# A two-layer hybrid encoder in split fp32r products: one PSUM bank per turned memory column, later casts for the second memory layer, split scores for the memory heads

## The chip, the cores and the metric

The kernel runs on one core of one Trainium2 chip. The metric is the device time of one execution in microseconds (us), the median of the runs shown. The core has a matrix engine (TensorE, PE; its weight loads appear as PEld), a vector engine (VectorE, DVE), an engine for activations and scaled copies (ScalarE, ACT), a general engine (GpSimd, POOL) and a sync engine that issues transfers (SyncE, SP). Each engine works through its own instructions in a fixed order. Matrix products are summed in PSUM, whose banks of 128 x 512 fp32 are the accumulators. DMA transfers move data between the chip's large memory and SBUF.

## What is computed

The reference is a trunk of two layers (DEPTH 2) over a sequence of 256 tokens of width 2048, with 256 memory tokens of the same width. What matters here of one layer:

```
proj = rmsnorm(x, norm_g[l]) @ w_in[l]            # split into conv, diff-attention and memory parts
y_a  = short_gated_conv(a_x, a_b, a_c, ...) * silu(a_g)
y_d  = headRMS(softmax(Q1 K1 / 8 + alibi) V - lam * softmax(Q2 K2 / 8 + alibi) V) * silu(d_g)   # 6 heads

mkv  = rmsnorm(mem, mem_norm_g[l]) @ w_mem_kv[l]  # 256 x 1024: keys | values
mk   = rmsnorm(mkv[..., :512] by heads of 128, mem_k_norm_g[l])
mv   = mkv[..., 512:] by heads of 128
mq   = rmsnorm(m_q by heads of 128, mem_q_norm_g[l])
y_m  = softmax(mq mk^T / sqrt(128)) mv * silu(m_g)                                              # 4 heads

x = x + concat(y_a, y_d, y_m) @ w_out[l]
```

All is fp32. The memory tokens are the same in both layers, so the keys and values of both can be made first.

## The kernel before

**Split products.** A large fp32 product is made of three products in fp32r, a shorter fp32 format with the size of fp32. Each operand is split into `hi`, its fp32r rounding (a cast on ACT), and `lo`, the rest (a subtraction on DVE). `products` (L298 to 304) then issues hi x hi, hi x lo and lo x hi for a 128 x 512 accumulator, 128 rows of the inner dimension at a time; the matmuls stand in L302. With two row tiles of 128 tokens that is six matmuls for each 128 x 512 piece of weights.

**Weights.** They arrive in `raw` tiles of 128 x 1024 (four buffers), are cast to `hi` and `lo` (four buffers each), and are read by PE. A buffer of `hi` and `lo` is free again when PE has done its products, a buffer of `raw` when DVE has made `lo`.

**The memory phase** comes first (class `Memory`, and the loop behind it). Its step s is layer l = s // 16 and inner tile k = s % 16: 0 to 15 are layer 0, 16 to 31 layer 1. A step has one `raw` tile of w_mem_kv: half 0 for the keys, half 1 for the values. Both halves and both row tiles make four accumulators, and the pool of accumulators has four banks, so layer 1's four are the banks of layer 0's four. `load` issues a step's transfer, `make` casts it: `hi` in L773 with the norm's gain as the scale, `lo` in L774. `times` runs the products. The loop takes steps in ones, and in pairs at k = 14, 15 and k = 0, 1, and makes the casts of the next steps ahead of a step's products.

When layer 0 is through, `keep_keys` (L872) copies the two key accumulators to `kraw` on ACT (L875), and `keep_values` (L878) copies the two value accumulators to `mv`, with a scale, on ACT (L880). Layer 1's first product into a bank has to wait for that bank's copy. The keys are then normed by pieces that run beside the next steps (squares in L359, the rest on DVE), turned by way of memory outside the core in `keys` (L718) into `mkT`, and multiplied there by the gain of the key norm, 128 x 1024 on ACT (L731).

Memory tokens come in rows and have to be turned: `rows_T` (L613) lets PE transpose two columns of 128 into one PSUM tile `pt` (L619), a bank, from a pool of two banks; `split_T` casts each column into `memT`, hi on ACT (L258), lo on DVE (L259). The first layer's steps do this; the second finds `memT` complete.

**What sets the order.** The framework orders each engine's instructions by its own simulated timeline, except those under `pin` (tc.keep_in_program_order), which stay in the order of the code relative to one another. Pinned are, among others, the copies of keys and values and the casts of steps up to 17 (`if s < KT + 2`, KT = 16). The casts of later steps are put where the framework's timeline has them.

**The layers** follow: per layer 14 blocks of 512 columns of w_in, then w_out. Each block takes its weights 128 x 1024 at a time ("chunk", 12 matmuls, about 2.7 us on PE). The small work runs beside the blocks as generators; `yield n` lets n chunks pass. The memory heads' queries are normed and turned into `mqT`, after which `turn_mq` marks the layer in `queries`. `mem_scores` (L589) waits for that mark and issues two fp32 matmuls for each head, `s<-mkT,mqT`, 128x256 (L595; the profile has two records for each). Softmax, the product with the values (L442, `po`), and a turn of the output by way of memory follow; `split_T` casts the outputs into `yT`, the stationary operand of w_out. The first two blocks of w_out start with the ten inner tiles of the diff and memory heads and take those of the convolution later.

The tile with tag `bgT` holds the turned gates of the convolution later in the layer; the tag has one buffer, and earlier in the layer the diff heads' second keys `k2` lie in it.

Of the kernel before, what the change touches and what calls it, by code (L numbers as in the profile page):

```python
# [10 lines left out]
F32 = mybir.dt.float32  # L11
F32R = mybir.dt.float32r
I32 = mybir.dt.int32
AF = mybir.ActivationFunctionType
ALU = mybir.AluOpType
# [3 lines left out]
P = 128  # L19
D_MODEL = 2048  # L20
SEQ = 256
DEPTH = 2
NT = SEQ // P
KT = D_MODEL // P
# [4 lines left out]
DH = W_DIFF // P  # L29
# [18 lines left out]
def encoder(ctx: ExitStack, tc: tile.TileContext, x, mem, norm_g, w_in, conv_w, conv_b,  # L48
            dq_g, dk_g, lq1, lk1, lq2, lk2, head_g, mem_norm_g, w_mem_kv, mq_g, mk_g, w_out, out):
    nc = tc.nc  # L50
    x, mem, out = x[0], mem[0], out[0]

    def pool(name, bufs, space=None):
        kw = {"space": space} if space is not None else {}
        return ctx.enter_context(tc.tile_pool(name=name, bufs=bufs, **kw))
# [4 lines left out]
    keep = pool("keep", 1)  # L60
# [5 lines left out]
    ps_t = pool("ps_t", 2, PSUM)  # L66
# [3 lines left out]
    def nm(s):  # L70
        uid[0] += 1
        return f"{s}_{uid[0]}"


    ident = const.tile([P, P], F32, name="ident")
# [59 lines left out]
    def g_mnorm(l, k):  # L135
        return cva[:, l * KT + k:l * KT + k + 1]
# [4 lines left out]
    mgain = const.tile([P, DEPTH], F32, name="mgain")  # L141
# [138 lines left out]
    def parts_tiles():  # L280
        return [wp.tile([P, CK, NB], F32R, tag=tag, name=nm(tag), bufs=PARTS // CK) for tag in ("hi", "lo")]
# [134 lines left out]
    def carry(sheet, to):  # L416


        d = dram.tile([NA, B, NA, sheet.shape[-1]], F32, name=nm("d"))
        for a in range(NA):  # L420
            tc.keep_in_program_order(nc.sync.dma_start(d[:, :, a].rearrange("b c r -> c b r"), sheet[a * B:(a + 1) * B]))
        yield 2
        of = d.rearrange("b c a (n i) -> (b c) a n i", i=B)
        for a in range(NA):
            tc.keep_in_program_order(nc.sync.dma_start(to[:, :, a], of[:, a]))
# [71 lines left out]
    scored = set()  # L497
# [3 lines left out]
    def pair(heads, begin, end, v):  # L501

        es = []
        for h in heads:
            while held["e"] == 2:
                yield 1
            held["e"] += 1
            es.append((yield from begin(h)))
            yield 2
        yield 4  # L510
        while held["sh"] == 2:
            yield 1
        held["sh"] += 1
        sh = tmp.tile([P, NA, 2, NT * NT, B], F32, tag="sh", name=nm("sh"))
        for i, e in enumerate(es):
            tc.keep_in_program_order(nc.vector.transpose(
                sh[:, :, i], e[0].rearrange("p t (k b c) -> p b (t k) c", k=NT, b=NA)))
            held["e"] -= 1
            yield 1
        yield 4  # L520
        flat = sh.rearrange("p b h n c -> p (b h n c)")
        yield from carry(sh.rearrange("p b h n c -> p b (h n c)"), flat.rearrange("p (n a i) -> p n a i", a=NA, i=B))
        eT = flat.rearrange("p (h t k q) -> p h t k q", h=2, t=NT, k=NT)
        while held["yn"] == 2:
            yield 1
        held["yn"] += 1
        yn = tmp.tile([P, NA, 2, NT, B], F32, tag="yn", name=nm("yn"))
        for i, h in enumerate(heads):
            end[0](h, yn[:, :, i], weighted(eT, i, v, h), *es[i][1:])
            yield 2  # L530
        held["sh"] -= 1
        yield 5
        tc.keep_in_program_order(nc.vector.transpose(yn, yn))
        yield 5
        flat = yn.rearrange("p b h t c -> p (b h t c)")
        yield from carry(yn.rearrange("p b h t c -> p b (h t c)"), flat.rearrange("p (n a i) -> p n a i", a=NA, i=B))
        for i, h in enumerate(heads):
            end[1](h, flat[:, i * SEQ:(i + 1) * SEQ])
            yield 1
        held["yn"] -= 1  # L540
# [43 lines left out]
            nc.vector.scalar_tensor_tensor(yn[:, :, i], strips(po[:, i, :]), r[:, i:i + 1],  # L584
                                           strips(a[:, i, h * P:(h + 1) * P]), ALU.mult, ALU.mult)

    queries = set()

    def mem_scores(l, h, qT, kT, st):  # L589
        while l not in queries:  # L590
            yield 1
        sc = P ** -0.5
        s = ps_s.tile([P, NT, SEQ], F32, tag="s", name=nm("s"))
        for i in range(NT):
            nc.tensor.matmul(s[:, i, :], qT[:, h, i * P:(i + 1) * P], kT[:, h, :], start=True, stop=True)  # L595
        mx = small.tile([P, NT], F32, tag="mmx", name=nm("mmx"))
        nc.vector.tensor_reduce(mx, s, AX.X, ALU.max)
        nc.vector.tensor_scalar(mx, mx, -sc, None, ALU.mult)
        sm = small.tile([P, NT], F32, tag="msm", name=nm("msm"))
        e = tmp.tile([P, NT, SEQ], F32, tag="e", name=nm("me"))  # L600
        for i in range(NT):
            nc.scalar.activation(e[:, i], s[:, i], AF.Exp, bias=mx[:, i:i + 1], scale=sc, accum_out=sm[:, i:i + 1])
        r = small.tile([P, NT], F32, tag="mr", name=nm("mr"), bufs=6)
        nc.vector.reciprocal(r, sm)
        nc.vector.tensor_tensor(r, r, st[:, HR], ALU.mult)
        return e, r
# [5 lines left out]

    def rows_T(src, k, n):  # L613

        pt = ps_t.tile([P, 2, SEQ], F32, tag="t", name=nm("pt"))
        for j in range(n):
            for t in range(NT):
                tc.keep_in_program_order(
                    nc.tensor.transpose(pt[:, j, t * P:(t + 1) * P], src(k + j, t), ident))  # L619
        return [pt[:, j, :] for j in range(n)]  # L620

    def strips_of(src):

# [62 lines left out]
    pin = tc.keep_in_program_order  # L686
# [31 lines left out]
    def keys(l, nat):  # L718


        d = dram.tile([NA, B, NA, W_MEM // P * NT * B], F32, name=nm("kd"))
        flat = nat.rearrange("p b j t c -> p b (j t c)")
        for a in range(NA):
            tc.keep_in_program_order(nc.gpsimd.dma_start(d[:, :, a].rearrange("b c r -> c b r"), flat[a * B:(a + 1) * B]))
        tc.keep_in_program_order(nc.gpsimd.dma_start(flat, d.rearrange("b c a r -> (b c) a r")))
        yield 8
        tc.keep_in_program_order(nc.vector.transpose(
            mkT[l].rearrange("p j (t a i) -> p (j t) a i", t=NT, a=NA),
            nat.rearrange("p a j t c -> p (j t) a c")))
        yield  # L730
        tc.keep_in_program_order(nc.scalar.activation(mkT[l], mkT[l], AF.Copy, scale=mgain[:, l:l + 1]))  # L731

    def x_natural(q):
        pin(nc.sync.dma_start(xs[:, :, q * NB:(q + 1) * NB],
# [2 lines left out]
    class Memory:  # L737
# [20 lines left out]
        def make(self, s):  # L758
            if s in self.parts:
                return  # L760
            self.load(s)
            l, k = divmod(s, KT)
            raw, (hi, lo) = self.raw.pop(s), parts_tiles()
            self.parts[s] = hi, lo
            if l == DEPTH:
                both = (nc.scalar.copy(hi, raw), nc.vector.tensor_tensor(lo, raw, hi.bitcast(F32), ALU.subtract))
                if k < 2:
                    for i in both:
                        pin(i)
                return  # L770
            g = g_mnorm(l, k)
            for j in (range(2) if s < 2 else (slice(0, 2),)):
                both = (nc.scalar.activation(hi[:, j], raw[:, j], AF.Copy, scale=g),  # L773
                        nc.vector.scalar_tensor_tensor(lo[:, j], raw[:, j], g, hi[:, j].bitcast(F32),  # L774
                                                       ALU.mult, ALU.subtract))
                if s < KT + 2:
                    for i in both:
                        pin(i)

# [5 lines left out]
        def begin(self, half, part, w):  # L785

            if part == 0 and w == 0:
                self.acc[0, half] = accumulators()
            w_part = self.parts[0][w][:, half]
            for t in range(NT):  # L790
                pin(nc.tensor.matmul(self.acc[0, half][t], memT[:, part, 0, t * P:(t + 1) * P], w_part,  # L791
                                     start=part == 0 and w == 0, stop=False))
# [15 lines left out]
    mkT, mv, stm, away = [], [], [], []  # L808
# [80 lines left out]
    s = 1  # L889
    while s < DEPTH * KT:  # L890
        l, k = divmod(s, KT)
# [22 lines left out]
        s = group[-1] + 1  # L914

    for l in range(DEPTH):
        st = stats_of(ssx, "st")
# [11 lines left out]
        def begin_pair(n, p):  # L929
            tasks.append(later(p, max(1, start + PAIR_EVERY * n - chunk[0])))  # L930
# [4 lines left out]
        for b in order:  # L935
# [7 lines left out]
            if b == 4:  # L943
                start = chunk[0]
# [18 lines left out]
        mqT = keep.tile([P, MH, SEQ], F32, tag="mqT", name=nm("mqT"))  # L963
# [2 lines left out]

        def turn_mq(nat):
            yield from turn_sheet(nat, mqT)
            queries.add(l)

        tasks.append(later(turn_mq(normed(acc, P, st, sheets("bgx"))), 8))
        acc = x_block([(C_M + W_MEM, NB)])
# [4 lines left out]
            split_T(yT, CG + DH + h, y, None, pin=True)  # L977

        for n in range(MH // 2):
            begin_pair(DH // 2 + n, pair((2 * n, 2 * n + 1), lambda h: mem_scores(l, h, mqT, mkT[l], st),  # L980
                                         (lambda h, yn, po, r: mem_out(h, yn, po, r, mga), mem_done), mv[l]))


# [1 line left out]
        bgT = None  # L985
# [78 lines left out]
        for b in range(4):  # L1064
# [3 lines left out]
            for t in range(NT):  # L1068
                n = 256 if final else NB
# [41 lines left out]
```

## Time and profile before

| | us |
|---|---|
| runs: 928.17, 926.55, 927.01; median | 927.01 |
| the profiled execution | 929.68 |
| its span, first to last instruction | 927.9 |
| PE busy in it | 919.7 |
| DVE busy | 668.2 |
| ACT busy | 495.1 |
| matmuls on memory tokens, layer 1's first to the first on xT | 57.48 to 103.14 |

The profile is of one execution. A row of the timeline has the start and duration in us, the engine, the line of the kernel, the operation with output <- input by the program's names, the shape, a count, and in brackets the idle time of the engine before it with what ended that. Rows of the groups have a count, the busy time and the mean of one in ns. Matmuls overlap: the time between the starts of two is what counts, not the duration of one. "PEclk" is the clock that TensorE was granted, as a share of full speed. A table of waits has, for each pair of waiting line and releaser, the us in total, how often, and the longest.

### The profile page before, as it was taken

To read this page: it belongs to the slowest core of one execution; us is meant where nothing else is said; L and a number is where in the kernel's file an instruction comes from. 1 tells how busy PE (TensorE), PEld (TensorE's weight loads), DVE (VectorE), ACT (ScalarE), POOL (GpSimd) and SP (SyncE) were. 2 spreads that over 40 slices of the span, in tenths; PEclk is the share of its full clock that TensorE was granted. 3 is DMA by queue.
4 is the path that set the end of the run, shared out by engine and by line. 5 is a ranking of instruction groups with operands and counts; after the bars stand their busy time and mean duration, and the time that the engine had idled before them with its cause. 6 is when DMAs were issued, how large, how long until landed. Compare 5 with 4: busy or idle time off the path is not lost.

```text
span 927.9 us, 12263 instructions
## 1 busy us (share of the span) xinstructions
PE 919.7 (99%) x4168; PEld 763.6 (82%) x4168; DVE 668.2 (72%) x1176; ACT 495.1 (53%) x751; POOL 36.5 (4%) x66
## 2 busy tenths in 40 slices
PE   9989999999999999999999999999999999999998
PEld 6878888888888888888888888888888888888886
DVE  5569887857798786567666757878898777558652
ACT  5657645576454554445555544568554554446431
POOL 2335010000000000000000000000000000000000
PEclk9999999999999999999999999999999999999999
DMA  8888777875679998988587766886889879988662
GB/s 282 283 241 245 247 260 229 248 227 182 197 209 227 259 253 240 251 256 255 204 279 244 233 192 219 241 234 181 246 230 220 261 210 259 248 236 240 211 218 74
DMA packets 247023, 215.10 MB, mean 232 GB/s; under 512 B 132131, under 2 KB 172913, under 8 KB 246961
## 3 DMA queue, kind: packets, MB, share of 16 engines
q1 hardware_dynamic: 242080, 208.71, 76.2%
q0 software_dynamic: 3680, 4.56, 2.3%
q10 hardware_dynamic: 1200, 1.07, 0.4%
q8 instruction: 32, 0.52, 0.2%
q14 instruction: 31, 0.25, 0.1%
HBM read 193.26 MB, written 20.97 MB: 231 GB/s over the span
## 4 chain that ended last, share of the span: by engine, by line
PE 97%; DMA 2%; DVE 1%; ACT 1%; issue 0%; SPq 0%; DVEq 0%; ACTq 0%
PE acc L302 92%; PE po L442 2%; DMA raw<-in_w_mem_kv_dram 2%; PE s L595 1%; PE s L550 1%; PE s L549 1%; PE acc L791 1%; DVE lo L774 0%; ACT hi L773 0%; PE pt L619 0%; ACT msq L698 0%; ACT kraw L875 0%; DVE memT L259 0%; SPq L689 0%; DVE xs L1072 0%
## 5 line engine op out<-in xcount | busy, mean ns | idle before, releaser
L302 PE MATMUL acc<-hi,xT 128*128 128x512 f32 x1792 | 561.2, 391 | 0.0
L291 ACT CAST hi<-raw 128x1024 fp32r<-128x1024 f32 x280 | 294.4, 1052 | 342.8 <-PE acc L302 284.3
L292 DVE TENSOR_TENSOR lo<-raw,hi 128x1024 fp32r<-128x1024 f32 x280 | 341.9, 1222 | 182.2 <-ACT hi L291 177.0
L302 PEld LDWEIGHTS acc<-hi,xT 128*128 128x128 f32 x1792 | 336.7, 188 | 68.7
L302 PE MATMUL acc<-lo,xT 128*128 128x512 f32 x896 | 349.3, 390 | 0.0
L302 PEld LDWEIGHTS acc<-lo,xT 128*128 128x128 f32 x896 | 168.5, 188 | 33.9
L302 PE MATMUL acc<-hi,yT 128*128 128x512 f32 x512 | 158.0, 389 | 0.0
L302 PEld LDWEIGHTS acc<-hi,yT 128*128 128x128 f32 x512 | 96.2, 188 | 19.8
L302 PE MATMUL acc<-lo,yT 128*128 128x512 f32 x256 | 99.7, 389 | 0.0
L302 PE MATMUL acc<-hi,memT 128*128 128x512 f32 x248 | 78.4, 399 | 2.4 <-ACT kraw L875 2.4
L302 PEld LDWEIGHTS acc<-hi,memT 128*128 128x128 f32 x248 | 46.9, 191 | 12.4 <-ACT kraw L875 2.8
L302 PEld LDWEIGHTS acc<-lo,yT 128*128 128x128 f32 x256 | 48.1, 188 | 10.0
L774 DVE SCALAR_TENSOR_TENSOR lo<-raw,cva,hi 128x1024 fp32r<-128x1024 f32 (+1 forms) x34 | 40.9, 1219 | 15.9 <-ACT hi L773 15.5
L302 PE MATMUL acc<-lo,memT 128*128 128x512 f32 x124 | 46.9, 394 | 0.0
L773 ACT ACTIVATE hi<-raw,cva 128x1024 fp32r<-128x1024 f32 (+1 forms) x34 | 36.2, 1095 | 11.9 <-DMA raw<-in_w_mem_kv_dram 8.8
L302 PEld LDWEIGHTS acc<-lo,memT 128*128 128x128 f32 x124 | 23.7, 192 | 5.0
L560 ACT ACTIVATE e<-e,mx 128x256 f32<-128x256 f32 x48 | 23.8, 498 | 1.4 <-DVE mx L556 1.3
L636 POOL DMA_DIRECT2D xt<-in_x_dram x32 | 21.5, 678 | 20.1 <-DVE rsa L186 14.9
L404 DVE STREAM_TRANSPOSE sh<-sh 128x1024 f32<-128x1024 f32 (+2 forms) x14 | 17.3, 1238 | 0.0
L554 DVE SCALAR_TENSOR_TENSOR e<-dist,s 128x512 f32<-128x512 f32 x24 | 15.7, 679 | 2.2 <-PE s L550 1.7
L261 ACT ACTIVATE xT<-xf,gx 128x256 fp32r<-128x256 f32 x32 | 14.4, 502 | 4.1 <-DVE xf L642 3.5
L1072 DVE TENSOR_TENSOR xs<-acc,xs 128x256 f32<-128x256 f32 (+1 forms) x24 | 10.9, 504 | 7.8 <-PE acc L302 7.8
(161 smaller groups left out, 581.7 us busy)
## 6 DMA issues: line engine op xcount, KB each, us to landing
raw<-in_w_in_dram SPq DMA_DIRECT2D x192, 512.0 KB, 4.4
raw<-in_w_out_dram SPq DMA_DIRECT2D x64, 512.0 KB, 4.4
raw<-in_w_in_dram SPq DMA_DIRECT2D x64, 256.0 KB, 4.1
raw<-in_w_mem_kv_dram SPq DMA_DIRECT2D x30, 512.0 KB, 5.9
d<-sh SPq DMA_DIRECT2D x80, 128.0 KB, 3.8
sh<-d SPq DMA_DIRECT2D x64, 128.0 KB, 4.3
d<-yn SPq DMA_DIRECT2D x40, 64.0 KB, 3.8
yn<-d SPq DMA_DIRECT2D x40, 64.0 KB, 3.7
```

The source lines that it names most:

```text
L261: both = (nc.scalar.activation(hi, src, AF.Copy, scale=gain), nc.vector.scalar_tensor_tensor(lo, src, gain, hi.bitcast(F32), ALU.mult, ALU ...
L291: nc.scalar.copy(hi, raw)
L292: nc.vector.tensor_tensor(lo_, raw, hi.bitcast(F32), ALU.subtract)
L302: i = nc.tensor.matmul(acc, left, right, start=start, stop=stop)
L404: tc.keep_in_program_order(nc.vector.transpose(src, src))
L442: nc.tensor.matmul(po[:, t, :], eT[:, i, t, k, :], v[:, k, h * P:(h + 1) * P], start=k == 0, stop=k == NT - 1)
L554: nc.vector.scalar_tensor_tensor(e[:, c], dist, -slopes[h], s[c], ALU.mult, ALU.add)
L560: nc.scalar.activation(e[:, c, i], e[:, c, i], AF.Exp, bias=mx[:, c, i:i + 1], accum_out=sm[:, c, i:i + 1])
L636: tc.keep_in_program_order(nc.gpsimd.dma_start(st[:, n], src[n * B:(n + 1) * B].rearrange("p (b r) -> b p r", b=NA)))
L773: both = (nc.scalar.activation(hi[:, j], raw[:, j], AF.Copy, scale=g), nc.vector.scalar_tensor_tensor(lo[:, j], raw[:, j], g, hi[:, j].bit ...
L774: nc.vector.scalar_tensor_tensor(lo[:, j], raw[:, j], g, hi[:, j].bitcast(F32), ALU.mult, ALU.subtract))
L1072: nc.vector.tensor_tensor(xc, acc[t][:, lo:lo + n], xc, ALU.add)
```

## The change

It has three parts.

1. `rows_T` takes one PSUM tile, a bank, for each turned column, instead of one for two columns. The pool still has two banks.
2. The casts of steps 18 and 19 are pinned too (`s < KT + 4`). In the order of the code they stand behind the copies of keys, where before the framework was free to put step 18's ahead of them.
3. The memory heads' scores. `keys` no longer multiplies `mkT` by the gain. `mem_scores` splits each head's query and key: `qh` by a copy on ACT, `ql` by a subtraction on DVE, `kh` by a copy scaled with the gain on ACT, `kl` by one instruction on DVE, 128x256 each, all pinned. One chunk later it issues six fp32r matmuls (qh x kh, qh x kl, ql x kh for two row tiles) where two fp32 matmuls stood. The pieces lie in a new tile `parts` with the tag `bgT`: two sets for queries, one for keys, so that a head's key casts wait for the score matmuls of the head before. `parts` waits until the diff heads' scores have read `k2`, and the turned gates wait for `parts`.

```diff
-    queries = set()
-
-    def mem_scores(l, h, qT, kT, st):
+    queries = {}
+
+    def mem_scores(l, h, st):
         while l not in queries:
             yield 1
+        qT, parts = queries[l]
+        q, k, g = qT[:, h], mkT[l][:, h], mgain[:, l:l + 1]
+        qh, ql, kh, kl = (parts[:, j] for j in (2 * (h % 2), 2 * (h % 2) + 1, 4, 5))
+        pin(nc.scalar.copy(qh, q))
+        pin(nc.vector.tensor_tensor(ql, q, qh.bitcast(F32), ALU.subtract))
+        pin(nc.scalar.activation(kh, k, AF.Copy, scale=g))
+        pin(nc.vector.scalar_tensor_tensor(kl, k, g, kh.bitcast(F32), ALU.mult, ALU.subtract))
+        yield 1
         sc = P ** -0.5
         s = ps_s.tile([P, NT, SEQ], F32, tag="s", name=nm("s"))
         for i in range(NT):
-            nc.tensor.matmul(s[:, i, :], qT[:, h, i * P:(i + 1) * P], kT[:, h, :], start=True, stop=True)
+            at = slice(i * P, (i + 1) * P)
+            nc.tensor.matmul(s[:, i, :], qh[:, at], kh, start=True, stop=False)
+            nc.tensor.matmul(s[:, i, :], qh[:, at], kl, start=False, stop=False)
+            nc.tensor.matmul(s[:, i, :], ql[:, at], kh, start=False, stop=True)
...
     def rows_T(src, k, n):
 
-        pt = ps_t.tile([P, 2, SEQ], F32, tag="t", name=nm("pt"))
-        for j in range(n):
+        pts = [ps_t.tile([P, SEQ], F32, tag="t", name=nm("pt")) for _ in range(n)]
+        for j, pt in enumerate(pts):
             for t in range(NT):
-                tc.keep_in_program_order(
-                    nc.tensor.transpose(pt[:, j, t * P:(t + 1) * P], src(k + j, t), ident))
-        return [pt[:, j, :] for j in range(n)]
+                tc.keep_in_program_order(nc.tensor.transpose(pt[:, t * P:(t + 1) * P], src(k + j, t), ident))
+        return pts
...
             nat.rearrange("p a j t c -> p (j t) a c")))
-        yield
-        tc.keep_in_program_order(nc.scalar.activation(mkT[l], mkT[l], AF.Copy, scale=mgain[:, l:l + 1]))
...
-                if s < KT + 2:
+                if s < KT + 4:
                     for i in both:
                         pin(i)
...
         def turn_mq(nat):
             yield from turn_sheet(nat, mqT)
-            queries.add(l)
+            assert all((l, d) in scored for d in range(DH))
+            queries[l] = mqT, keep.tile([P, 6, SEQ], F32R, tag="bgT", name=nm("parts"))
...
-            begin_pair(DH // 2 + n, pair((2 * n, 2 * n + 1), lambda h: mem_scores(l, h, mqT, mkT[l], st),
+            begin_pair(DH // 2 + n, pair((2 * n, 2 * n + 1), lambda h: mem_scores(l, h, st),
```

Lines behind the edits carry higher numbers afterwards: L773 becomes L781, L774 L782, L875 L883, L880 L888.

The order of ACT around the end of layer 0, before. The numbers behind the names count buffers: hi_550 and hi_554 are steps 16 and 17, hi_612 step 18, hi_616 step 19; acc_155 and acc_156 are layer 0's keys, acc_174 and acc_175 its values.

```order
L773 ACTIVATE hi_550<-raw_502,cva 128x1024
L773 ACTIVATE hi_554<-raw_535,cva 128x1024
L773 ACTIVATE hi_612<-raw_587,cva 128x1024
L875 COPY kraw_570<-acc_155 128x512
L875 COPY kraw_570<-acc_156 128x512
L880 ACTIVATE mv_111<-acc_174,stm 128x512
L880 ACTIVATE mv_111<-acc_175,stm 128x512
L359 ACTIVATE sq_601<-kraw_570 128x512
L773 ACTIVATE hi_616<-raw_598,cva 128x1024
```

And with the change, where hi_557 and hi_561 are steps 16 and 17, hi_619 step 18 and hi_623 step 19:

```order
L781 ACTIVATE hi_557<-raw_508,cva 128x1024
L781 ACTIVATE hi_561<-raw_542,cva 128x1024
L883 COPY kraw_577<-acc_155 128x512
L883 COPY kraw_577<-acc_156 128x512
L359 ACTIVATE sq_608<-kraw_577 128x512
L888 ACTIVATE mv_111<-acc_174,stm 128x512
L359 ACTIVATE sq_610<-kraw_577 128x512
L781 ACTIVATE hi_619<-raw_594,cva 128x1024
L888 ACTIVATE mv_111<-acc_175,stm 128x512
L781 ACTIVATE hi_623<-raw_605,cva 128x1024
```

Step 18's cast has moved behind both copies of keys, and the copies of values stand behind the squares of the keys, the second behind step 18's cast too.

PE at the first memory head's scores of layer 0, before (the name of the weights' buffer tells the chunk):

```order
L302 MATMUL acc_2672<-hi_2859,xT_109 128x512
L302 MATMUL acc_2672<-lo_2860,xT_109 128x512
L302 MATMUL acc_2672<-hi_2859,xT_109 128x512
L595 MATMUL s_2884<-mkT_110,mqT_2155 128x256 x2
L302 MATMUL acc_2671<-hi_2899,xT_109 128x512
```

And with the change, where hi_2896 is the chunk that hi_2899 is above:

```order
L302 MATMUL acc_2677<-lo_2897,xT_109 128x512
L302 MATMUL acc_2677<-hi_2896,xT_109 128x512
L604 MATMUL s_2912<-parts_2889 128x256
L605 MATMUL s_2912<-parts_2889 128x256
L606 MATMUL s_2912<-parts_2889 128x256
L604 MATMUL s_2912<-parts_2889 128x256
L605 MATMUL s_2912<-parts_2889 128x256
L606 MATMUL s_2912<-parts_2889 128x256
L302 MATMUL acc_2931<-hi_2936,xT_109 128x512
```

The scores are six instructions instead of two and stand one chunk, 12 matmuls, later.

## The prediction, as put on record

> **What bounds the kernel now.** I read the page first: its busy times and its chain of work that ended last.
>
> ```profile
> PE 919.7 (99%) x4168; PEld 763.6 (82%) x4168; DVE 668.2 (72%) x1176; ACT 495.1 (53%) x751; POOL 36.5 (4%) x66
> PE 97%; DMA 2%; DVE 1%; ACT 1%; issue 0%; SPq 0%; DVEq 0%; ACTq 0%
> ```
>
> TensorE (PE) is busy for 919.7 of 927.9 us and is 97% of the chain. So only three things can change the time: fewer or shorter matmuls, less idle time of PE, or a higher granted clock. The second view is the table of waits, for PE alone; it is complete:
>
> ```profile
> PE acc L302 <- ACT kraw L875: 2.4, 1, 2.4
> PE warm L123 <- DVE zeros L118: 1.2, 1, 1.2
> PE acc L791 <- ACT hi L773: 0.7, 1, 0.7
> ```
>
> The last two lie in the first microseconds, where the change does nothing. The first is one wait for a copy of keys, which the change moves. The third view is the table by windows around it, whose columns after the window's length are PE, PEld, DVE, ACT and POOL busy time, then the granted clock, the DMA share and GB/s.
>
> ```profile
> 45.00:55.00 10.00, 10.00 (x47) 8.03 (x45) 8.55 (x22) 4.46 (x6) 8.62 (x13) 1.00 0.94 200
> 57.48:61.69 4.21, 4.21 (x11) 3.33 (x12) 1.71 (x3) 3.03 (x5) 0.00 (x0) 0.59 1.07 311
> 61.69:65.00 3.31, 3.31 (x16) 2.77 (x15) 2.83 (x8) 0.92 (x3) 0.00 (x0) 1.00 0.83 321
> 65.00:85.00 20.00, 20.00 (x90) 16.59 (x89) 18.72 (x31) 17.38 (x33) 11.65 (x18) 1.00 0.73 197
> 85.00:95.00 10.00, 10.00 (x45) 7.96 (x45) 9.13 (x22) 5.65 (x9) 1.88 (x4) 1.00 1.00 320
> ```
>
> The second row begins where PE resumes: the granted clock is 0.59 for 4.21 us, in which 11 matmuls run, and 1.00 again after that. The wait thus costs more than itself. The fourth view, the timeline from 49 to 62 us, shows how it comes about (start, duration, engine, line, operation, idle time before it and releaser):
>
> ```profile
> 49.67 0.37 ACT L258 CAST memT<-pt 128x256 fp32r<-128x256 f32 x1 [2.36 <-DVE memT L259]
> 49.94 3.24 ACT L773 ACTIVATE hi<-raw,cva 128x1024 fp32r<-128x1024 f32 x3
> ...
> 54.72 0.39 PE L302 MATMUL acc<-hi,memT 128*128 128x512 f32 x1
> 55.81 1.15 ACT L773 ACTIVATE hi<-raw,cva 128x1024 fp32r<-128x1024 f32 x1 [2.63 <-DMA raw<-in_w_mem_kv_dram]
> 56.86 1.05 ACT L875 COPY kraw<-acc 128x512 f32<-128x512 f32 x2
> ...
> 57.48 0.50 PE L302 MATMUL acc<-hi,memT 128*128 128x512 f32 x1 [2.37 <-ACT kraw L875]
> 57.80 1.28 ACT L880 ACTIVATE mv<-acc,stm 128x512 f32<-128x512 f32 x2
> 58.95 0.65 ACT L359 ACTIVATE sq<-kraw 128x512 f32<-128x512 f32 x1
> 60.78 1.15 ACT L773 ACTIVATE hi<-raw,cva 128x1024 fp32r<-128x1024 f32 x1 [1.18 <-DMA raw<-in_w_mem_kv_dram]
> ```
>
> ACT runs in order. The cast of step 18 (55.81) stands ahead of the first copy of keys, and its raw weights land only then, after 2.63 us of waiting. The copy therefore starts at 56.86, although PE had ended the accumulator it reads six matmuls before its last one at 54.72, at about 53.7. Layer 1's first product needs that bank and waits until 57.48.
>
> **The change, part by part.** First the pace of PE, from the chain of waits and a timeline of the scores:
>
> ```profile
> 23.22 5.49 PE acc L302 x24
> 305.91 0.86 PE s L595 x4
> 716.25 0.87 PE s L595 x4
> 276.01 0.28 PE L549 MATMUL s<-yT 128*128 128x256 f32 x1
> 276.94 0.39 PE L302 MATMUL acc<-lo,xT 128*128 128x512 f32 x1
> ```
>
> A product of 512 columns takes 5.49/24 = 0.229 us. A memory head's scores take 0.86 to 0.87 us (four records). Between the last two rows lie the eight fp32r score matmuls of a diff head, 128x256 each: 0.93/8 = 0.116 us apiece.
>
> *The casts of steps 18 and 19, moved behind the copies.* By the order that the change gives ACT, the copies follow the casts of steps 15 to 17, which end at 49.94 + 3.24 = 53.18. The first copy can then start when PE is through with its bank, about 53.8, and is done by 54.4, the second by 55.0. PE ends its previous matmul at 54.95 and meets a free bank. The 2.37 us go, and with them the slow stretch: 11 x 0.229 = 2.52 at full pace instead of 4.21, another 1.69. Together **-4.06 us**. What is late next: the two copies of values now stand behind one square each (0.65) and, the second, behind the cast of step 18. From 55.0: square to 55.6, values to 56.2, square to 56.8, cast to 58.0, values to 58.6. PE, counted along its new order at 0.229, wants the third bank at 57.7, step 18's high part at 59.1, and the fourth bank at 59.8. All three are there, by 1.1 us or more.
>
> *Own banks.* The pair of casts of two turned columns no longer alternates between ACT and DVE in one bank. The page of waits gives what that alternation costs now:
>
> ```profile
> ACT memT L258 <- DVE memT L259: 5.3, 7, 2.4
> ACT hi L291 <- PE acc L302: 284.3, 183, 3.0
> ```
>
> That is 5.3 us of ACT's idle time in seven places, none on PE's path by itself, so I give it nothing directly. The long one (2.36, at 49.67) does delay the casts of steps 15 to 17, their low parts, the raw buffers that these free, and so the next loads; without it they come up to about 1.3 us earlier (the DVE work ahead keeps the rest). Both new banks of a pair must be empty before the next pair is turned: by the next rows the pairs lie 5.9 us apart, and even the late one is through 4.2 us after it begins (50.08 + 0.42 - 46.30).
>
> ```profile
> 40.39 0.60 PE L619 MATMUL pt<-ident,xs 128*128 128x128 f32 x4
> 46.30 0.60 PE L619 MATMUL pt<-ident,xs 128*128 128x128 f32 x4
> ...
> 50.08 0.42 DVE L259 TENSOR_TENSOR memT<-pt,memT 128x256 fp32r<-128x256 f32 x1 [0.44 <-ACT memT L258]
> ```
>
> *Scores from split operands.* Each head's scores become six matmuls of the diff heads' shape and type: 6 x 0.116 = 0.70 instead of 0.866, so 0.17 less, eight times: **-1.35 us**. Above, a 256-column product could cost what a 512-column one does (0.229): 6 x 0.229 = 1.37, or +4.0 us over eight heads; below, half of that, 0.114, which is nearly the row I take, since it has the same shape. The Trainium skill, in "FP8 and Floating Point Precision", section "TensorE Precision Notes", counts four passes for a true fp32 matmul; three of four would leave 0.65 of 0.866 and save 1.7 us, against 1.35 by the row.
>
> The added casts are 16 on ACT and 16 on DVE, 128x256 each; two scalings of 128x1024 on ACT go:
>
> ```profile
> L258 ACT CAST memT<-pt x16: 372/372/375, 4.0 to 49.7; 128x256 fp32r<-128x256 f32 x16
> L259 DVE TENSOR_TENSOR memT<-pt,memT x16: 419/425/426, 4.4 to 50.1; 128x256 fp32r<-128x256 f32 x16
> L261 ACT ACTIVATE xT<-xf,gx 128x256 fp32r<-128x256 f32 x32 | 14.4, 502 | 4.1 <-DVE xf L642 3.5
> L731 ACT ACTIVATE mkT<-mkT,mgain x2: 1154/1156/1157, 110.1 to 150.8; 128x1024 f32<-128x1024 f32 x2
> ```
>
> ACT gains 16 x 0.37 - 2.31 = 3.6 us, or 16 x 0.50 - 2.31 = 5.7 if each takes the 0.50 of xT's; DVE 16 x 0.42 = 6.8. I cost them at nothing: ACT spends 284.3 us waiting for PE to free a buffer, casts run three buffers (36 matmuls, 8 us) ahead, and a head's four casts delay the next weight cast by under 1 us. Without that cover each head would cost up to 0.9 us. Three waits are new. The first query cast needs the turned queries, the second head's keys need the first head's score matmuls, and the memory outputs come later:
>
> ```profile
> 301.56 1.05 ACT L291 CAST hi<-raw 128x1024 fp32r<-128x1024 f32 x1 [3.10 <-DVE rsa L200]
> 416.67 0.40 ACT L258 CAST yT<-yn 128x256 fp32r<-128x256 f32 x1
> 426.40 0.39 PE L302 MATMUL acc<-hi,yT 128*128 128x512 f32 x1
> ```
>
> At the first place ACT is idle for 3.10 us anyway, and the scores stand 12 matmuls (2.7 us) later on PE than before. Behind the second stands a weight cast whose product lies 59 matmuls (13.5 us) behind the scores waited for. Third, by the orders the last memory pair is weighted 48 matmuls (11.0 us) later; its cast now ends at 417.1, and w_out reads that column 48 matmuls after 426.40, at 437.4. Of 20.3 us, 9.3 are left. None stops PE.
>
> *What eats into the gain.* PE comes to layer 1's later steps 4.06 us earlier, where the loads and DVE, by the windows above, are nearly full (DVE 18.72 of 20 from 65 to 85, DMA 1.00 from 85 to 95). Two places in that stretch, and its end:
>
> ```profile
> 78.67 2.47 DVE L774 SCALAR_TENSOR_TENSOR lo<-raw,cva,hi 128x1024 fp32r<-128x1024 f32 x2
> ...
> 93.69 1.16 ACT L773 ACTIVATE hi<-raw,cva 128x1024 fp32r<-128x1024 f32 x1 [0.20 <-DMA raw<-in_w_mem_kv_dram]
> 95.33 1.28 DVE L774 SCALAR_TENSOR_TENSOR lo<-raw,cva,hi 128x1024 fp32r<-128x1024 f32 x1
> ...
> 103.14 0.39 PE L302 MATMUL acc<-hi,xT 128*128 128x512 f32 x1
> ```
>
> Step 31's low part is ready at 96.6. The first product of layer 1 now starts at 54.95, and the order puts 177 matmuls ahead of the one that reads this low part: 54.95 + 177 x 0.229 = 95.5. If loads and casts kept their times PE would wait 1.1 us there; step 24's low part, the first of the two at 78.67, is ready at 79.9 and wanted 100 matmuls in, at 77.9, 2.0 us too early. With the buffers freed up to 1.3 us earlier, 0 to 0.8 remains, over both places. I take **+0.6**, between nothing and about 1.3.
>
> **Sum:** -4.06 - 1.35 + 0.6 = -4.8 us. The profiled execution was 929.68 us, 927.9 of it span, so a profiled one would show 924.9. The runs' median is 2.67 lower: 927.01 - 4.8 = **922.2 us**.
>
> **Rivals.**
>
> *The slow stretch stays.* If the granted clock falls here for a reason other than the gap (some load on the chip at that time, or a count over a longer stretch of work), the 1.69 us are not gained: -4.8 + 1.69 = -3.1, so 923.9. For it: the 0.59 is one event, seen once. Against it: it begins at the very matmul that ends the gap, with 1.00 before and after. The Trainium skill ("TensorE: Matmul & The Clock Gate", section "Why this matters for your kernels") says that PE gaps up to about 3 us don't drop the clock; by that rule a gap of 2.37 would not be the cause and this rival would hold. The trace has 0.59 behind such a gap, which speaks against the rule without proving the cause.
>
> *The gain runs into the stretch from 62 to 96 us.* Transfers and DVE keep their times and PE waits once or twice, 1.1 to 2.0 us, perhaps with a slow stretch of 1 us after it: 2 to 3 us come back instead of 0.6, so 923.6 to 924.6. For it: the two late low parts above. Against it: the cast chain starts earlier, and the freed buffers with it.
>
> *The change doesn't do what it says.* The copies still end late, or the wait goes to the values' banks, and only the scores gain: 927.01 - 1.35 = 925.7. Against it: the margins of 1.1 us.
>
> *Slower: the last memory outputs become late for w_out.* They pass through score matmuls, softmax, two turns through memory and a cast ahead of which PE can't take the last columns. If the chain from the split to the output is longer by more than 9.3 us over the 11.0 that the order moves it, PE waits at 437 and again at the same place in layer 1. Two waits of 3 us, each with 1.69 us of slow clock behind it, are 9.4: 922.2 + 9.4 = 931.6. It takes two of 1.7 us to pass 928.9. For it: the path has six hand-overs that the order alone doesn't time. Against it: nearly as much slack as is used up.
>
> **How the numbers follow.** A measurement of this kernel can tell about 0.2%, 1.85 us, from no change. Forecast, with 921.2 to 923.2 as its own range: 0.56. Slow stretch stays: 0.08. Late casts: 0.16. Only the scores: 0.08. Slower: 0.12. Faster than 925.2 are the first three: 0.80. Only the scores is within 0.2%: 0.08. Slower: 0.12. The range goes from 920.6 (no give-back and the larger saving at the scores, -4.06 - 1.7 is 921.3, and the scatter of 0.5 to 1 us of the runs shown) to 925.8, which takes in all cases but the slower one.
>
> **What would show it.** Right: no wait of PE for kraw and a granted clock of 1.00 from 55 to 65; groups of six score matmuls of 0.70 us each; the first product on xT, now at 103.14, at 99.1 to 100.2; no wait of PE on parts or yT. The give-back would stand as waits of PE on lo or hi of L782 and L781 between 62 and 96. Wrong: the same wait under another name (mv, hi of step 18), a clock under 1.00 without a gap ahead, score groups above 0.87, or PE waiting for yT near 437 and 850.

## The result, and the profile after

Timed side by side, six runs each, the changed kernel takes 923.75 us (923.66 to 924.33) and the kernel before 928.24 (926.55 to 929.05). The ratio is 0.9956, with a 95% interval of 0.9943 to 0.9969: 4.5 us less. The forecast was 922.2, with a range of 920.6 to 925.8 and a gain of 4.8. The profiled execution of the changed kernel was 923.66 us.

The page of the changed kernel, its busy times and the engines of the chain that ended last:

```profile
PE 916.2 (99%) x4184; PEld 760.6 (83%) x4184; DVE 670.0 (73%) x1192; ACT 498.2 (54%) x765; POOL 36.7 (4%) x66
PE 99%; ACT 0%; DVE 0%; issue 0%; DVEq 0%
```

TensorE's share of the chain rose from 97 to 99%, and the DMA, 2% before, has left it. The waits of PE, again complete:

```profile
PE warm L123 <- DVE zeros L118: 1.2, 1, 1.2
PE acc L302 <- DVE lo L782: 0.3, 1, 0.3
PE acc L799 <- ACT hi L781: 0.2, 1, 0.2
```

The wait for `kraw` is gone. One of 0.3 us for a low part has come, but it lies among the first products of layer 0 and not behind the old gap:

```profile
9.91 0.50 PE L302 MATMUL acc<-lo,memT 128*128 128x512 f32 x1 [0.27 <-DVE lo L782]
```

The windows around the old gap (columns as before, the clock is the third from the end):

```profile
45.00:55.00 10.00, 10.00 (x48) 8.26 (x47) 7.40 (x19) 5.79 (x9) 7.15 (x11) 1.00 1.01 235
57.48:61.69 4.21, 4.21 (x20) 3.51 (x19) 2.78 (x7) 1.16 (x1) 0.00 (x0) 1.00 1.04 351
```

Where 11 matmul records stood in 4.21 us at a clock of 0.59, there are 20 now, at 1.00. The timeline of ACT, and behind it the first product on xT and the start of a head's scores on PE:

```profile
53.10 1.07 ACT L883 COPY kraw<-acc 128x512 f32<-128x512 f32 x2 [2.93 <-PE acc L302]
54.06 0.65 ACT L359 ACTIVATE sq<-kraw 128x512 f32<-128x512 f32 x1
54.59 0.69 ACT L888 ACTIVATE mv<-acc,stm 128x512 f32<-128x512 f32 x1
55.16 0.64 ACT L359 ACTIVATE sq<-kraw 128x512 f32<-128x512 f32 x1
55.68 1.16 ACT L781 ACTIVATE hi<-raw,cva 128x1024 fp32r<-128x1024 f32 x1
56.72 0.70 ACT L888 ACTIVATE mv<-acc,stm 128x512 f32<-128x512 f32 x1
57.58 1.16 ACT L781 ACTIVATE hi<-raw,cva 128x1024 fp32r<-128x1024 f32 x1 [0.16 <-DMA raw<-in_w_mem_kv_dram]
...
98.21 0.39 PE L302 MATMUL acc<-hi,xT 128*128 128x512 f32 x1
...
303.53 0.28 PE L604 MATMUL s<-parts 128*128 128x256 f32 x1
...
304.25 0.39 PE L302 MATMUL acc<-hi,xT 128*128 128x512 f32 x1
```

The copies now wait for PE and not the other way round. A head's scores take 304.25 - 303.53 = 0.72 us, 0.71 in the chain of waits, instead of 0.86. The last product of layer 0 and the twelfth of layer 1 start on PE at:

```profile
54.03 0.61 PE L302 MATMUL acc<-hi,memT 128*128 128x512 f32 x2
...
56.75 0.61 PE L302 MATMUL acc<-hi,memT 128*128 128x512 f32 x2
```

That is 2.72 us from one to the other. Before it was 61.69 - 54.72 = 6.97, so the place of the old gap is 4.25 us shorter.

So the profiled times differ by 929.68 - 923.66 = 6.0 us, more than the medians do. From the first product on memory tokens to the first on xT by the timelines it was 103.14 - 5.46 = 97.68 us, and is 98.21 - 5.06 = 93.15: 4.5 less. Of these 4.5, 4.25 are the place of the old gap. Some 0.3 lie in layer 0, from its first product to its last (49.26 us before, 48.97 now); the clock rose to full at 7.50 us in this execution and at 10.30 in the one before, which may be why. The first weights happened to come 0.4 earlier. The last 1.1 us lie behind the first product on xT, where the scores are. So about 0.7 of the 6.0 us belong to the start of these two executions and not to the change.

### The profile page after: what moved, and what is told of

It reads as the page before. It is cut to its first block, busy times and chain, and to the rows that moved or that the text cites. A ratio compares the mean times of both kernels' runs of the same rounds, so it can differ in the third digit from the quotient of the medians.

```text
span 921.9 us, 12335 instructions
## 1 busy us (share of the span) xinstructions
PE 916.2 (99%) x4184; PEld 760.6 (83%) x4184; DVE 670.0 (73%) x1192; ACT 498.2 (54%) x765; POOL 36.7 (4%) x66
## 4 chain that ended last, share of the span: by engine, by line
PE 99%; ACT 0%; DVE 0%; issue 0%; DVEq 0%
PE acc L302 94%; PE po L442 2%; PE s L550 1%; PE s L549 1%; PE pt L629 0%; PE acc L799 0%; PE s L606 0%; PE s L604 0%; PE s L605 0%; PE warm L123 0%; ACT hi L781 0%; DVE lo L782 0%; DVE xs L1081 0%; ACT memT L258 0%; DVEq L1115 0%
## 5 line engine op out<-in xcount | busy, mean ns | idle before, releaser
L782 DVE SCALAR_TENSOR_TENSOR lo<-raw,cva,hi 128x1024 fp32r<-128x1024 f32 (+1 forms) x34 | 41.0, 1219 | 15.0 <-ACT hi L781 14.8
L781 ACT ACTIVATE hi<-raw,cva 128x1024 fp32r<-128x1024 f32 (+1 forms) x34 | 36.6, 1099 | 10.7 <-DMA raw<-in_w_mem_kv_dram 6.4
```

## The experiments

The first four kernels take the change apart, each timed with the kernel before on the same chip; that kernel's 35 runs there had a median of 929.17 us and went from 925.66 to 932.32.

**One line: the casts of steps 18 and 19 pinned.**

```diff
-                if s < KT + 2:
+                if s < KT + 4:
```

> The kernel before with one line changed: the casts of steps 18 and 19 are pinned behind the copies. Theory (the gap causes the slow stretch): no wait of PE for kraw, granted clock 1.00 from 55 to 65 us, and about 3.3 us less than before, which is the whole gain of 4.5 less 1.2 for the scores. Rival 1 (the slow stretch has another cause): the wait is gone but a stretch of some 4 us with a clock near 0.6 stays, and the gain is about 2. Rival 2 (the shared bank delays the casts of steps 15 to 17 enough for the gain to run into late casts): PE waits for hi or lo between 62 and 96 us, 1 to 2 us in all, and the gain is 1 to 2.

Measured: 925.68 us (924.89 to 926.39), ratio 0.9973 [0.9961, 0.9985]. The wait for kraw is gone and the clock is 1.00 from 45 to 95 us. PE waits for a low part, 0.5 us. The gain against before is 2.5 us by the ratio and 3.5 by the medians. Rival 1 fell: no slow stretch without the gap, and all twelve runs have a mean clock of 0.999 or more. Of rival 2 there are 0.5 us, at 78.10.

**One bank for each turned column, nothing else.** The edit is that of `rows_T` in the change.

> The kernel before with one bank for each turned column, nothing else. The cast of step 18 still stands ahead of the copies and still waits for its weights. Theory: the low parts that free the raw buffers come up to 1.3 us earlier, so do step 18's weights, and the wait for kraw falls from 2.4 to 1.1 or more, with the slow clock behind it as long as the gap is there: 0 to 2.5 us less than before. Rival: the load is late for its own reasons (queue), the wait stays at 2.4 and the time is the same within 0.5 us.

Measured: 926.51 us (925.88 to 929.83), ratio 0.9985 [0.9970, 1.0001]. The surprise is in its profile: without any pin, the wait for kraw is gone from the table. ACT's timeline of this kernel:

```profile
49.91 1.15 ACT L772 ACTIVATE hi<-raw,cva 128x1024 fp32r<-128x1024 f32 x1 [0.23 <-PE acc L302]
53.60 1.15 ACT L772 ACTIVATE hi<-raw,cva 128x1024 fp32r<-128x1024 f32 x1 [2.53 <-DMA raw<-in_w_mem_kv_dram]
54.66 1.05 ACT L874 COPY kraw<-acc 128x512 f32<-128x512 f32 x2
```

Step 18's cast still waits for its weights ahead of the copies, but these weights land at about 53.5 us and not at 55.7, and the first copy is done about when PE comes. Counted from the last product of layer 0 on PE (54.93 here, 54.72 in the kernel before, 53.35 in the next kernel, which shares banks too), step 18's cast starts 1.3 us before it here, and 1.1 and 1.2 us behind it in the other two. That the buffers freed sooner bring the load forward is the argument of the prediction; it fits, but no run takes it apart. Two of the twelve runs lie about 3 us above the median, with a mean clock of 0.998; there the weights may have been late again, which was not profiled. So this part and the pin are two cures of one wait, and their gains don't add up. The pin takes the dependence on the load away; the banks only bring the load forward.

**The split scores alone.** The edits are those of `mem_scores`, `keys`, `turn_mq` and the call in the change.

> The kernel before with the memory heads' split scores alone. Theory: eight groups of six matmuls of 0.12 us, 0.71 to 0.72 each instead of 0.86 to 0.87, so 1.2 us less; the wait for kraw and the slow stretch as before, 2.4 and about 1.7 us. Rival: the casts or the later memory outputs make PE wait, and the gain is nothing or less.

Measured: 927.12 us (925.83 to 929.50), ratio 0.9988 [0.9974, 1.0002]. By the ratio that is 1.1 us, where 1.2 was expected; the interval just includes nothing. Sorted by mean clock, which the runs further down call for, it is 0.9 us among the runs over 0.998 (median 926.24 against 927.12) and 1.3 among the others (928.62 against 929.89). Its profile has the wait for kraw as before, 2.5 us, and a slow stretch behind it, at another time than in the kernel before (56 and not 58 us). No wait of PE hangs on the new casts.

**The change with two columns in a bank.**

> The change without its first part: two turned columns share a bank again. Theory: the own banks matter only for how early the later casts come; PE then waits longer for lo or hi between 62 and 96 us than the 0.3 us of the change, 0.5 to 1.5 us, and the kernel is slower than the change by that. Rival: the earlier casts are worth nothing, and the time is that of the change, 4.5 us less than before.

Measured: 924.73 us (923.80 to 925.94), ratio 0.9953 [0.9939, 0.9967]. The change, run again in a later group (below), had 924.35, its first six runs 923.75. It has a wait for a low part where the change has none, at step 24 of the memory phase:

```profile
78.41 0.50 PE L302 MATMUL acc<-lo,memT 128*128 128x512 f32 x1 [0.56 <-DVE lo L783]
```

The kernel with the pin alone has the same wait, 0.47 us at 78.10. The 0.3 us of the change, with which the expectation compares, lie at 9.91 us and have nothing to do with it. So the own banks take away this wait of about half a microsecond. By the medians they bring 0.4 to 1.0 us beside the pin, which the intervals don't separate from nothing.

**How long must a gap be?** The slow clock stood behind a gap in each of two profiles (the kernel before and the scores alone). The next kernels are the change with a gap made on purpose, of a length that no load decides: the first copy of keys is repeated, and PE waits for the last.

```diff
-            pin(nc.scalar.copy(kraw[:, t], m.acc[l, 0][t]))
+            for _ in range(4 if l == 0 and t == 0 else 1):
+                pin(nc.scalar.copy(kraw[:, t], m.acc[l, 0][t]))
```

> The change with the first copy of keys made four times over (layer 0 alone), so that PE, ready at about 54.3 us, waits for the last of them until 53.1 + 4 x 0.53 + 0.06 = 55.3: a gap of about 1.0 us. Theory (the gap causes the slow clock, and a short one does not): the clock stays 1.00 and the span grows by 1.0. Rival (something else near 55 us slows the clock in the kernel before): the clock stays 1.00 here and behind longer gaps too.

With 5, 7 and 10 copies:

> As gap3 with the copy made five times: a gap of about 1.5 us. Theory: somewhere between 1 and 2.4 us of gap the slow stretch begins; if it does here, matmuls run at 0.38 to 0.45 us for about 4 us and another 1.7 us are lost; if not, 1.5 alone. Rival: 1.00 throughout.

> As gap3 with the copy made seven times: a gap of about 2.6 us, that of the kernel before, at another moment and beside other transfers. Theory: a slow stretch of about 4 us right behind the gap, granted clock 0.5 to 0.7 in it, some 1.7 us lost besides the 2.6. Rival: 1.00 behind the gap, 2.6 lost alone.

> As gap3 with the copy made ten times: a gap of about 4.2 us. Theory: the slow stretch behind it is of the same length and depth as behind 2.6, 4 us and 1.7 lost, if the length of the gap does not matter beyond the point where it begins. Rival: 1.00 behind the gap.

Measured, one execution each:

| copies | gap, us | mean clock | time, us |
|---|---|---|---|
| 4 | 1.2 | 1.000 | 925.85 |
| 5 | 1.8 | 1.000 | 926.33 |
| 7 | 3.0 | 1.000 | 927.58 |
| 10 | 4.9 | 0.995 | 931.08 |

The 3.0 us gap had no slow clock, although the 2.4 of the kernel before has one. That refutes a bound on the length alone, and with it the expectation for 7 copies. The one for 10 copies, a slow stretch of the same length whatever the gap, fell too. The windows of three kernels, cut within 0.05 us of where the clock changes, show more. First the kernel before (PE's busy time stands behind the window's length):

```profile
54.67:58.08 3.41, 1.04 (x5) 0.54 (x5) 1.56 (x2) 2.27 (x4) 0.00 (x0) 1.00 0.97 266
58.08:61.45 3.37, 3.37 (x10) 2.61 (x9) 1.11 (x3) 2.19 (x4) 0.00 (x0) 0.50 1.06 287
61.45:64.85 3.40, 3.40 (x16) 2.83 (x15) 2.71 (x7) 1.01 (x3) 0.00 (x0) 0.99 0.84 325
```

The same for the scores alone:

```profile
52.36:55.77 3.41, 1.38 (x7) 0.80 (x5) 1.49 (x3) 1.24 (x2) 0.89 (x2) 0.99 1.01 190
55.77:59.14 3.37, 2.94 (x7) 2.36 (x8) 1.97 (x3) 3.28 (x6) 0.00 (x0) 0.50 1.06 254
59.14:62.50 3.36, 3.36 (x16) 2.73 (x16) 2.89 (x8) 0.95 (x2) 0.00 (x0) 1.00 1.03 377
```

And for ten copies:

```profile
53.83:57.24 3.41, 0.65 (x3) 0.19 (x1) 0.00 (x0) 3.25 (x6) 0.00 (x0) 1.00 1.08 289
57.24:60.65 3.41, 1.31 (x3) 1.11 (x4) 0.00 (x0) 3.31 (x7) 0.00 (x0) 0.50 1.04 275
60.65:64.06 3.41, 3.41 (x9) 2.64 (x9) 2.52 (x4) 3.40 (x5) 0.00 (x0) 0.50 0.11 44
64.06:67.40 3.34, 3.34 (x16) 2.72 (x16) 2.46 (x8) 0.75 (x1) 0.00 (x0) 1.00 0.54 186
```

The clock is 0.50 or 1.00, nothing between, and changes at steps of about 3.4 us: the slow stretch is one such step in the first two and two steps in the third. In each case PE was idle for 2.0 to 2.8 us of the step just before a slow one (3.41 - 1.38 = 2.03 is the least). In the kernel before, the clock falls at 58.08, 0.6 us after PE has resumed, so it doesn't fall as soon as a gap has reached some length. This suggests that the clock is judged step by step, by a count that runs without regard to the kernel, so that the same gap costs more or less by where it falls. The Trainium skill ("TensorE: Matmul & The Clock Gate", section "What's actually happening") describes a free-running window of about 3.4 us, and the trace agrees with that length. It has the clock fall after an idle window, where here 2.0 us of 3.4 sufficed. The next two runs test whether the place of the gap decides.

**The same gaps, timed.** These are the kernels of 5 and 7 copies again.

> The kernel with five copies and a PE gap of 1.8 us that hangs on ACT alone, timed. Theory (the clock is judged in stretches of about 3.4 us that run by themselves, and falls for the next stretch where PE was idle for some 2 us or more of one): 1.8 never suffices, so all runs lie in one group within about 1 us, 2 to 2.5 us above the change. Rival (the clock falls by the length of the gap alone, above some bound over 3 us): the same here.

> The kernel with seven copies and a gap of 3.0 us, timed. Its one profile had no slow stretch although the gap is longer than the 2.4 before which has one. Theory (stretches of 3.4 us with their own phase): in some runs the gap is split over two stretches and costs 3 us alone, in others it falls largely into one and costs some 1.7 us more: runs in two groups, about 3.5 and 5 us above the change. Rival (length alone): one group, 3 to 3.8 above the change.

Measured, with the runs sorted by the mean clock that each lists (one step of 3.4 us at half the clock in 926 us makes a mean of 0.998):

| kernel | clock over 0.998 | clock 0.998 or less |
|---|---|---|
| 5 copies, gap 1.8 us | 5 runs, median 926.11 | 7 runs, median 928.04 |
| 7 copies, gap 3.0 us | 4 runs, median 927.40 | 8 runs, median 929.17 |
| before, in this group | 13 runs, median 927.47 | 11 runs, median 929.97 |
| before, in the first group | 15 runs, median 927.12 | 20 runs, median 929.89 |

Both kernels fall into two groups, 1.8 to 1.9 us apart, with an identical program whose gap had one length in both of its profiles. That is what the theory of the phase says for 3.0 us. For 1.8 us it was wrong: this gap was expected never to suffice, and the clock fell in 7 of 12 runs.

The traces allow a closer look. In the record of the clock of all fourteen profiles, every complete stretch is a whole number of steps of 3.413 us long, from the first rise to full clock on: in the kernel before 14 steps at full clock (10.30 to 58.08), one at half, 254 at full. So the steps can be counted on from the first rise where the clock doesn't change, too. Here are the steps that hold the gap, with 5 copies (first row) and with 7 (the other two), from the first profile of each:

```profile
53.55:56.96 3.41, 1.62 (x8) 1.05 (x7) 0.00 (x0) 3.22 (x6) 0.68 (x1) 1.00 1.00 253
...
53.38:56.79 3.41, 1.65 (x8) 1.03 (x6) 0.00 (x0) 2.93 (x5) 0.00 (x0) 1.00 1.04 266
56.79:60.21 3.42, 2.16 (x9) 1.80 (x10) 0.01 (x1) 3.38 (x7) 0.00 (x0) 1.00 1.06 304
```

The same count for every profile with a gap there:

| profile | gap, us | PE idle in the steps of the gap, us | clock of the step behind each |
|---|---|---|---|
| 4 copies | 1.2 | 1.17 | 1.00 |
| 5 copies | 1.8 | 1.79 | 1.00 |
| 5 copies, second profile | 1.8 | 1.40 and 0.39 | 1.00 and 1.00 |
| 7 copies | 3.0 | 1.76 and 1.25 | 1.00 and 1.00 |
| 7 copies, second profile | 3.0 | 1.49 and 1.53 | 1.00 and 1.00 |
| scores alone | 2.5 | 1.99 and 0.47 | 0.50 and 1.00 |
| before | 2.4 | 2.37 | 0.50 |
| 10 copies | 4.9 | 2.76 and 2.11 | 0.50 and 0.50 |

All of them fit one rule: a step is run at half the clock when PE was idle for some 2 us of the step before it. The end of the kernels, where PE runs out of work, bears it out. Over all steps of all fourteen profiles from the first rise on, each with 1.99 us or more of idle time is followed by a clock of 0.50, and none with 1.93 or less is (the 1.93 stand from 920.37 to 923.78 in the first profile of 7 copies). Both profiled gaps of 3.0 us were split over two steps, so the phase explains why they cost nothing more. The rule leaves the 7 slow runs of 5 copies open: a gap of 1.8 us can't put 1.99 into one step. The gap may have been longer in those runs, or the count may not be PE's idle time as the profile has it; none of them was profiled.

**The change again, and the scores later.** The last kernel lets two chunks pass between a head's casts and its scores.

```diff
-        yield 1
+        yield 2
         sc = P ** -0.5
```

> The change, unaltered, timed and profiled again beside the other kernels of this group. Theory: with no wait of PE that hangs on a late load, its runs lie within 1 us of each other, where those of the kernel before lie within 6; no wait for kraw and a clock of 1.00. Rival: the small spread of the first six runs was luck.

> The change with the scores issued two chunks behind their casts instead of one: the last of them move by 48 matmuls, 10.9 us, and with them the memory outputs, which in the change are cast by 424.7 with w_out reaching them at 433. Theory (the memory outputs have 8 to 9 us of slack): PE waits for yT about 2 us in each layer, or the framework hides part of it by putting the second block's products first: 0 to 5 us slower than the change. Rival (they have much more slack): no wait, the same time.

Measured: the change again 924.35 us (923.39 to 925.20), ratio 0.9951 [0.9931, 0.9970]; every run has a clock above 0.998. They spread over 1.8 us, more than the first six did and more than expected, but the kernel before spread over 5.9 in this group. With later scores: 924.65 us (923.67 to 925.47), ratio 0.9954 [0.9937, 0.9972], and no wait of PE for yT. The last memory output is cast at 422.44 in the change, where w_out reaches it at about 432:

```profile
422.44 0.40 ACT L258 CAST yT<-yn 128x256 fp32r<-128x256 f32 x1
```

With later scores it is cast 17 us later than that:

```profile
431.48 0.41 ACT L258 CAST yT<-yn 128x256 fp32r<-128x256 f32 x1 [0.98 <-DMA yn<-d]
439.59 0.40 ACT L258 CAST yT<-yn 128x256 fp32r<-128x256 f32 x1
```

The two medians lie 0.3 us apart, within the scatter, so it cost nothing that shows. From about 432 us on, PE's products with yT stand in another order than in the change: the framework moved others ahead of those that need the late outputs. The expectation had named this way out, the second block's products first, beside its 2 us a layer, which did not come. How late the outputs may come before PE stops was not found. No version tried was faster than the change.

## Why the prediction was right, and where its numbers were off

**The bound** (PE, by chain and waits): right. What the profiles show as gained by the change came out of one gap, the clock behind it, and shorter score matmuls: 4.25 + 1.1 = 5.3 us, against the 4.8 of the sum.

**The casts behind the copies**, -4.06 us: right for the profiled execution, where the place of the gap and the slow stretch shrank by 4.25 us. The pin alone does it. The margins were near what was worked out: the first copy starts at 53.10 (said: 53.8), step 18's cast at 55.68 (56.8), with PE 0.7 us earlier than before at the end of layer 0. For the same reason the first product on xT, at 98.21, came before the 99.1 to 100.2 that were said.

**The slow stretch as part of the gain:** right in kind, and wrong as a constant of the kernel. This is the step that failed: "The runs' median is 2.67 lower: 927.01 - 4.8". The profiled execution of 929.68 had the stretch; of the kernel before, 31 of 59 runs in the two groups above had a clock of 0.998 or less, and 28 did not. The three runs shown, 926.55 to 928.17, all lie within the span of the runs without it (925.66 to 928.77); their own clock is not on record. The forecast thus subtracted 1.69 us from a median that very likely did not hold it. Taking the sum from the profiled time alone gives 924.9, against 923.66 and, in the second profile of the change, 924.5. Not knowing that the stretch comes and goes is very likely also why 922.2 lies 1.6 us under the 923.75 measured. That the gain of 4.8 nearly came out, at 4.5, is in part luck: it holds for a mix of runs. Within the later group the change's median is 3.1 us below the runs of the kernel before with a clock over 0.998, and 5.6 below the others.

**The rival that the stretch stays** had a chance of 0.08 and was refuted by the kernel with the pin alone: no gap, and no slow clock in any of twelve runs. The rule that was put beside it, that gaps up to about 3 us don't matter, failed in this case at 1.8 us in 7 of 12 runs, and held at 3.0 in 4 of 12.

**Own banks**, nothing directly and earlier casts: the runs agree. Without them PE waits half a microsecond at step 24. What was missed is that step 18's own weights come earlier, too, by 2 us, enough to close the gap in the profiled execution of the banks alone.

**Scores**, -1.35 us: 0.71 us a head instead of the 0.70 said, so 8 x 0.15 = 1.2. By runs it was 1.1, with an interval that includes nothing. The price of 0.116 for a 256-column matmul was 0.12. The casts cost nothing, as said. The wait for the queries on ACT was 1.5 us, and hit no one.

**Give-back**, +0.6: nothing. Between 62 and 96 us PE waits for no cast in either profile of the change. The place was right, since PE does wait at step 24's low part, by 0.5 to 0.6 us, in the two kernels with the pin and a shared bank; the own banks cover it whole. One sign of it is step 19's cast, which waits for its weights in both kernels: it starts at 57.58 and not at 60.78.

**Memory outputs late for w_out**, 9.3 us of slack: in the change the last high part is ready at 422.8 and wanted at about 432, 9 us. That it would decide beyond that was wrong: outputs 17 us later cost nothing, and the framework had given PE's products another order.

## What to carry to other kernels

A gap of the matrix engine is priced by its length and by what the clock does behind it; look at the granted clock in windows of about 3.4 us around each wait, and time both kernels often enough to see whether the runs fall into groups. A sum made on one profiled execution holds for that execution: before carrying it to a median, ask whether the event that is removed happened in the runs behind the median. In an engine that works in order, a cast whose load may be late should not stand ahead of the copy that frees an accumulator; bringing the load forward kept the clock up in 10 of 12 runs here, changing the order in all 43 runs of the kernels that have it and no gap made on purpose.

## What the runs showed of the hardware

From its first rise on, the granted clock of TensorE was 0.50 or 1.00, and in all fourteen profiles it changed only at whole multiples of 3.413 us from that rise. In these profiles every step of that length with 1.99 us or more of PE idle time was followed by one at 0.50, and none with 1.93 us or less was. One step at half the clock cost 1.7 to 1.9 us. By their mean clock, whether a gap of 1.8 or 3.0 us was followed by one varied from run to run of the same program. A gap of 4.9 us, run once, cost two steps.

Three fp32r matmuls of 128x256 took 0.36 us in place of one fp32 matmul of 0.43. The fp32 one thus costs about 3.6 of them.
